# Delta rule with the inverse inside the scan, TensorE's order from an estimate of engine times, decays made in each batch

## The chip, the cores and the metric

The kernel runs on one core of one Trainium2 chip. The metric is device time in microseconds (us), the median of several executions. Five engines work side by side, each through its own queue in order: TensorE (PE, matmuls; its weight loads are shown as PEld), VectorE (DVE), ScalarE (ACT), GpSimd (POOL) and SyncE (SP, which here only issues DMAs).

## The reference: what is computed

Two layers over 1088 frames (1024 of a prompt, 64 of a running sample), width 1024, one set of weights. The even layer is a gated convolution beside chunk-band attention, the odd layer a gated DeltaNet with 8 heads of 128; each ends in an output projection, a norm and a residual sum. The change is in the odd layer's recurrence over chunks of 64 frames, and in the order of everything on TensorE.

```python
def gdn_chunk(S, q, k, v, g, beta):
    gc = jnp.cumsum(g, axis=1)
    decay = jnp.exp(jnp.where(incl, gct[..., :, None] - gct[..., None, :], -jnp.inf))
    kk = jnp.einsum('blhd,bmhd->bhlm', k, k)
    a = jnp.where(strict, bt[..., :, None] * kk * decay, 0.0)
    tmat = a + jnp.eye(L)
    rhs = concatenate([v * beta, k * (beta * jnp.exp(gc))])
    sol = triangular_solve(tmat, rhs, lower=True, unit_diagonal=True)
    u = sol[..., :HD_C] - jnp.einsum('bhlk,bhkv->bhlv', sol[..., HD_C:], S)
    qk = jnp.einsum('blhd,bmhd->bhlm', q, k) * decay
    o = jnp.einsum('blhk,bhkv->blhv', q * jnp.exp(gc), S) + jnp.einsum('bhlm,bhmv->blhv', qk, u)
    k_dec = k * jnp.exp(g_last - gc)
    S_new = jnp.exp(g_last) * S + jnp.einsum('blhk,bhlv->bhkv', k_dec, u)
    return S_new, o
```

## The kernel before

**Projections.** Weights come as 128-column tiles (`wf`, two DMAs of 256 KB each on SP's queue) and are split into a high and a low part (`whi` by ACT, line 161; `wlo` by DVE, line 162). `project` (line 172) runs, for each of the three groups of frames (384, 384, 320 columns) and each of eight slices of the width, three matmuls in the reduced-precision format fp32r on the whole 128 x 128 array; their output is the PSUM tile `pjt`. The program makes 5832 of these. Everything else on TensorE is plain fp32, of which the trace shows two records per matmul and one per transpose.

**The odd layer.** Heads go in four pairs. A pair's q, k and v columns are six weight tiles; `conv` (line 699) convolves them into `kq` and `vt`, two buffers each, so the projections of pair p wait until the scan of pair p-2 has ended (line 1168). The 17 chunks of a pair go in three batches of 6, 6 and 5. Per batch:

- `prepare` (855): loads the decays `Dst` and `DT` from DRAM (lines 869 and 870, SP's queue), transposes k and q, takes norms, and forms the strict matrix `An` and the masked product `KQD`.
- `substitute` (918): inverts the 16 x 16 diagonal blocks on POOL: 28 small steps (lines 930 and 931) between two trips through DRAM (`Sd` to `AL`, then `AL` to `Sd`).
- `join` (938): reads the blocks back (`Xf`), and builds the 64 x 64 inverse with matmuls of 16 and 32 columns on 32 x 32 corners of the array, each pair of heads into the block-diagonal `BD`.
- `solve` (1006): per chunk a transpose of v, a product of `kt` with `BD` and one of `BD` with v, all on the whole array.
- `scan` (1032): per chunk `ks` (four matmuls, weights of 64 columns: k and q of both heads against the state `S`), `us` on DVE, `su` (two matmuls over 64 rows), the new `S` on DVE, and later `up` (two matmuls on 64 x 64 corners) for the output.

Before all this `decays` (821) makes the decay matrices of all 12 batches, two POOL and two ACT steps and two stores to DRAM each, in a buffer `dbuf` that shares the two places of `vt`; the projections of pair 1 therefore stop at the line `yield "decays"` (1175) until all twelve are made.

**Order.** TensorE's instructions run in the order in which the program writes them. `Order` (line 75) holds the work as generators with a rank; it always takes the ready one of lowest rank (scan 1, solve 1.3, join 1.5, substitute 1.6, prepare 2, decays and the final norms 3, projections 5). A generator that has to wait for other engines yields a fixed number of nanoseconds; the clock against which this runs adds up estimated matmul times only. The order on the other engines is made by the compiler's scheduler.

Of the kernel before, what the change touches and what calls it, by code (L numbers as in the profile page):

```python
# [1 line left out]

# [13 lines left out]
P = 128  # L16
# [15 lines left out]
NBM = 6  # L32
# [41 lines left out]

class Order:
# [4 lines left out]
    def __init__(self):  # L80
        self.now = 0.0
        self.live = []
        self.done = set()

    def add(self, name, rank, steps, after=()):
        self.live.append([rank, len(self.live), name, steps, 0.0, set(after)])

    def run(self):
        while self.live:
            self.live.sort(key=lambda t: t[:2])  # L90
            free = [t for t in self.live if not (t[5] - self.done)]
            ready = [t for t in free if t[4] <= self.now]
            if not ready:
                self.now = min(t[4] for t in free)
                continue
            t = ready[0]
            try:
                w = next(t[3])
                if isinstance(w, str):
                    t[5].add(w)  # L100
                else:
                    t[4] = self.now + w
# [5 lines left out]
class Net:  # L108
    def __init__(self, tc, I, O):
        self.tc, self.nc, self.I, self.O = tc, tc.nc, I, O  # L110
        self.pe, self.act, self.dve, self.pool = tc.nc.tensor, tc.nc.scalar, tc.nc.vector, tc.nc.gpsimd
        self.order = Order()


    def mm(self, out, lhsT, rhs, start=True, stop=True, share=1, **k):
        n = out.free_size()
        four = 1 if lhsT.dtype == F32R else 4
        self.order.now += max(n, 60 if four == 1 else 16) * four / 2.4 / share + 3
        return self.pe.matmul(out, lhsT=lhsT, rhs=rhs, start=start, stop=stop, **k)  # L119

    def tr(self, out, in_):
        k = in_.partition_size()
        self.order.now += 108 if k > 64 else 56
        return self.pe.transpose(out, in_, self.ident[0:k, 0:k])  # L124

    def bank(self):
        p = self.banks[0]
        self.banks = self.banks[1:] + [p]
        return p.tile([P, 512], F32, name="pjt", tag="pj", bufs=2 if p is self.pj else 4)

# [41 lines left out]
    def project(self, w, ops, n, m=P, ks=range(KT)):  # L172

        ps = self.bank()
        ks = list(ks)
# [41 lines left out]
    def open(self, name, side="left", **k):  # L217
        es = ExitStack()
        p = es.enter_context(self.tc.tile_pool(name=name, bufs=1, **(dict(side=side, reuse_waits="tile") if not k else k)))
# [7 lines left out]
    def run(self):  # L227
# [4 lines left out]
        with tc.tile_pool(name="pj", bufs=2, space=PSUM) as self.pj:  # L232
# [15 lines left out]
            self.Dd = [dram.tile([P, NCH, 64], F32, name=f"Dd{i}") for i in range(8)]  # L248
# [44 lines left out]
    def norm(self, l, g, xin, y, acc, last):  # L293
# [4 lines left out]
        yield 1620  # L298
        r = self.rstd(tp, acc, n, None if l and g else last)
        yield 2500  # L300
        if l == 0:
            acc = tp.tile([P, GMAX], F32, name="sqb", tag="sqa", bufs=2)[:, :n]
        for m in range(KT):
# [11 lines left out]
            yield 1050  # L315
        if l == 0:
            nc.sync.dma_start(self.xd[:, :, t0:t0 + n], x[:, :, :n])
            yield 2500
            r = self.rstd(tp, [acc, sq], n, last)
            self.new_h(g)  # L320
            yield 2500
            for k in range(KT):
                self.h_tile(tp, 1, g, x, r, k)
                yield 1360
# [76 lines left out]
    def even(self):  # L401
# [7 lines left out]
        self.sc_free = 0.0  # L409
# [74 lines left out]
        def v_tokens(p):  # L484
            b = B[p]
            for i0, m in ((0, 4), (4, 4), (8, 1)):
# [785 lines left out]
```

## Time and profile before

| | us |
|---|---|
| median of 3 runs (lowest, highest) | 1501.44 (1500.14, 1503.16) |
| the profiled execution's own time | 1498.51 |
| its span, first to last instruction | 1496.7 |
| ACT whi, 222 casts / DVE wlo, 222 subtractions | 129.9 / 155.6 |
| scan matmuls of `ks` / `su` / `up`, busy | 42.7 / 33.5 / 29.6 |

The profile's windows give the time in which each engine worked in a stretch, and PEclk, the share of TensorE's full clock that was granted there. A wait names the instruction that ended it. Matmuls overlap: a row's busy time is the union of its records, so what one more matmul costs is read from the distance between starts in the timeline.

By the order of the program and the trace, the stages are: even layer to about 542 us (2304 projection matmuls), its output projection to about 652, the odd layer to about 1346, then the last gates and the output projection. The 68 chunks of the scan run from 834 to 1336, some 4.4 us apart where they follow one another.

### The profile page before, as it was taken

To read this page: it belongs to the slowest core of one execution; us is meant where nothing else is said; L and a number is where in the kernel's file an instruction comes from. 1 tells how busy PE (TensorE), PEld (TensorE's weight loads), DVE (VectorE), ACT (ScalarE), POOL (GpSimd) and SP (SyncE) were. 2 spreads that over 40 slices of the span, in tenths; PEclk is the share of its full clock that TensorE was granted. 3 is DMA by queue.
4 is the path that set the end of the run, shared out by engine and by line. 5 is a ranking of instruction groups with operands and counts; after the bars stand their busy time and mean duration, and the time that the engine had idled before them with its cause. 6 is when DMAs were issued, how large, how long until landed. Compare 5 with 4: busy or idle time off the path is not lost. (4 is left out here: it accounts for less than half of the span.)

```text
span 1496.7 us, 28755 instructions
## 1 busy us (share of the span) xinstructions
PE 1376.2 (92%) x10578; PEld 1237.4 (83%) x10578; DVE 858.7 (57%) x2400; ACT 745.6 (50%) x1948; POOL 402.1 (27%) x909
## 2 busy tenths in 40 slices
PE   4899999999999999898876999999989989999995
PEld 3888998999999899887765877778877778888985
DVE  6647237326525755776675667664756665443654
ACT  6544144235325456776655566556555644323642
POOL 4100000000000014432447254452645261410322
PEclk9999999999999999998987999999999999999998
DMA  5231210220211174541332112211211132337454
GB/s 201 83 114 44 77 58 26 87 65 29 74 61 58 44 233 149 180 146 36 94 87 63 31 51 57 42 41 47 67 35 41 37 96 60 99 108 238 154 190 156
DMA packets 114381, 133.15 MB, mean 89 GB/s; under 512 B 35568, under 2 KB 81336, under 8 KB 114240
## 3 DMA queue, kind: packets, MB, share of 16 engines
q1 hardware_dynamic: 82128, 101.86, 22.9%
q10 hardware_dynamic: 32112, 29.45, 6.1%
q8 instruction: 83, 1.36, 0.4%
q14 instruction: 58, 0.48, 0.1%
HBM read 99.91 MB, written 34.51 MB: 90 GB/s over the span
## 5 line engine op out<-in xcount | busy, mean ns | idle before, releaser
L119 PE MATMUL pjt<-hhi,wlo 128*128 128x384 f32 (+1 forms) x1768 | 621.4, 351 | 1.8 <-DVE wlo L162 1.8
L119 PE MATMUL pjt<-hhi,whi 128*128 128x384 f32 (+1 forms) x1768 | 587.5, 332 | 19.7 <-ACT ko L464 4.2
L119 PE MATMUL pjt<-hlo,whi 128*128 128x384 f32 (+1 forms) x1768 | 586.8, 332 | 7.3 <-DVE hlo L215 6.6
L119 PEld LDWEIGHTS pjt<-hhi,whi 128*128 128x128 f32 x1768 | 340.4, 193 | 29.1 <-ACT hhi L214 6.6
L119 PEld LDWEIGHTS pjt<-hhi,wlo 128*128 128x128 f32 x1768 | 340.3, 192 | 26.0 <-issue 12.2
L119 PEld LDWEIGHTS pjt<-hlo,whi 128*128 128x128 f32 x1768 | 339.0, 192 | 10.5 <-DVE hlo L215 8.8
L162 DVE TENSOR_TENSOR wlo<-wf,whi 128x512 fp32r<-128x512 f32 x222 | 155.6, 727 | 138.3 <-ACT whi L161 137.0
L161 ACT CAST whi<-wf 128x512 fp32r<-128x512 f32 x222 | 129.9, 619 | 154.7 <-PE pjt L119 110.9
L544 ACT ACTIVATE pr<-pr,mx 128x640 f32<-128x640 f32 (+5 forms) x72 | 50.9, 706 | 92.7 <-DVE mx L543 92.2
L722 POOL TENSOR_TENSOR kq<-kq,tap 128x384 f32<-128x384 f32 (+1 forms) x64 | 49.7, 784 | 140.5 <-DVE kq L719 99.5
L505 POOL MEMSET bias<- 64x64 f32 x8 | 1.5, 187 | 315.4 <-DMA bias<-Gd 245.0
L345 POOL TENSOR_TENSOR sqa<-sqa,sq 128x384 f32<-128x384 f32 (+1 forms) x36 | 39.7, 1103 | 150.1 <-ACT sq L343 150.0
L541 DVE CUSTOM_DVE_ANT_0 pr<-sc,bias 128x640 f32<-128x640 f32 (+5 forms) x72 | 48.0, 666 | 26.3 <-PE sc L119 22.8
L1093 DVE SCALAR_TENSOR_TENSOR S<-S,egl,su 128x128 f32<-128x128 f32 x128 | 41.1, 343 | 34.9 <-PE su L119 34.3
L930 POOL TENSOR_TENSOR px<-AL 48x14 f32<-48x14 f32 (+6 forms) x168 | 48.6, 289 | 40.0 <-DMA AL<-Sd 31.6
L931 POOL TENSOR_TENSOR AL<-AL,px 48x14 f32<-48x14 f32 (+6 forms) x168 | 52.4, 312 | 8.7
L719 DVE SCALAR_TENSOR_TENSOR kq<-raw,par,kq 128x384 f32<-128x384 f32 (+1 forms) x96 | 48.7, 526 | 9.9 <-ACT raw L715 9.7
L610 POOL TENSOR_TENSOR cvo<-cvo,th 128x384 f32<-128x384 f32 (+1 forms) x12 | 12.0, 999 | 142.6 <-DVE mx L543 113.3
L884 ACT ACTIVATE junk<-tr 128x128 f32<-128x128 f32 x136 | 38.0, 279 | 19.8 <-PE tr L124 16.5
L124 PE MATMUL pt<-cst,pr 128*128 128x128 f32 (+1 forms) x280 | 43.2, 270 | 4.4 <-DVE pr L546 2.9
L119 PE MATMUL pjt<-mhi,whi 128*128 128x384 f32 x128 | 43.5, 340 | 3.1 <-ACT mhi L161 3.1
L119 PE MATMUL pjt<-mlo,whi 128*128 128x384 f32 x128 | 43.7, 342 | 0.3 <-DVE mlo L162 0.3
(240 smaller groups left out, 2344.5 us busy)
## 6 DMA issues: line engine op xcount, KB each, us to landing
wf<-in_w_in SPq DMA_DIRECT2D x128, 256.0 KB, 3.2
wf<-in_w_out SPq DMA_DIRECT2D x96, 256.0 KB, 3.4
mf<-mixd SPq DMA_DIRECT2D x32, 192.0 KB, 3.5
x<-in_x SPq DMA_DIRECT2D x8, 384.0 KB, 5.3
xg<-in_x SPq DMA_DIRECT2D x2, 1536.0 KB
xd<-xg SPq DMA_DIRECT2D x2, 1536.0 KB, 6.9
Dd<-dbuf ACTq DMA_DIRECT2D x16, 192.0 KB, 2.2
od<-o ACTq DMA_DIRECT2D x12, 256.0 KB, 2.5
```

What stands on the lines that cost most here:

```text
L119: return self.pe.matmul(out, lhsT=lhsT, rhs=rhs, start=start, stop=stop, **k)
L124: return self.pe.transpose(out, in_, self.ident[0:k, 0:k])
L161: self.act.copy(out=hi, in_=x)
L162: (eng or self.dve).tensor_tensor(lo, x, hi.bitcast(F32), ALU.subtract)
L345: pool.tensor_tensor(acc, acc, sq, ALU.add)
L541: dve.tensor_tensor_reduce(out=cut(pr[0:nq, :nk]), in0=sc[0:nq, :nk // nw, :nw], in1=cut(b["bias"][a][0:nq, j0:j0 + nk]), scale=1.0, scala ...
L544: act.activation(pr[0:nq, :nk], pr[0:nq, :nk], AF.Exp, bias=mx[0:nq, 1:2], scale=1.0, accum_out=mx[0:nq, 2:3])
L719: dve.scalar_tensor_tensor(o, ch(raw[:, i0 + j:i0 + j + m]), cw[j], o, ALU.mult, ALU.add)
L722: pool.tensor_tensor(o, o, ch(t), ALU.add)
L930: pool.tensor_tensor(t, AL[:, j + 1:16, j:j + 1].broadcast_to([lanes, m, w]), x.broadcast_to([lanes, m, w]), ALU.mult)
L931: pool.tensor_tensor(o, o, t, ALU.add)
L1093: dve.scalar_tensor_tensor(Sn[:, q, :], S[:, q, :], egl[:, q, p, c:c + 1], su[q], ALU.mult, ALU.add)
```

## The change

1. **Order.** `Clock` replaces the fixed waits. While the program is recorded it is told of every instruction (`Meter` wraps the other engines, `Pool` the buffers), books it with a fixed and a per-column cost on its engine, and keeps for each part of a tile when it will be written or read for the last time. A generator now yields the tiles and buffer places that its next matmul needs and is ready when the estimate has passed them all, with 250 ns more for all but the projections. `project` yields between its matmuls too.
2. **Decays.** `decays`, its DRAM tensors `Dd`, the buffer `dbuf` and the stop of pair 1 go. `prepare` makes `Dst` and `DT` itself: the same matmul, two POOL and two ACT steps per batch. 24 stores on ACT's queue and 24 loads on SP's queue go.
3. **Solve.** `solve` goes; of it only the transpose of v is left (`values`). `join` makes the inverse in both orientations (`tr<-X,M` beside `tr<-M,X`), and a new product `tr<-KQD,Ti` on 64 x 64 corners, so that one matrix `MT` per chunk holds inverse and masked q-k product for both heads.
4. **Scan.** Three dependent matmul steps per chunk in place of two and a late one. `ks`: two matmuls on the whole array (k and q of one head stand side by side in `kq`). Then `r` (two DVE steps of 64 rows into a block-diagonal tile whose other half is zero), `uo` (one matmul of 256 columns), two ACT copies to the block-diagonal `u`, `su` (one matmul of 256 columns) and the new `S`. The output's first part is copied from `ks` by ACT, the second added from `uo` by DVE.

```diff
+class Clock:
...
+    FIXED = {"DVE": 170, "ACT": 210, "POOL": 260}
+    EACH = {"DVE": 1.04, "ACT": 0.84, "POOL": 1.9}
+    NEAR, PSUM, DMA, BYTES = 60, 190, 2000, 190.0
...
+    def tensor(self, out, ins, cost, shape, more):
+        t = max([self.now] + [self.ready(x) for x in ins] + ([] if more else [self.over(out, "PE", False)]))
+        if shape != self.shape:
+            t += 200
+            self.shape = shape
+        self.now = t + cost
...
+    def other(self, eng, op, outs, ins):
+        t = max([self.ready(x, eng) for x in ins] + [self.over(x, eng, False) for x in outs])
...
+            n = max(x.free_size() for x in outs[:1] + ins)
+            took = self.FIXED[eng] + self.EACH[eng] * n + (200 if len(outs) > 1 else 0)
+            at = self.place(eng, t, took)
...
 class Order:
...
+    LATE = 250
...
+    def due(self, t):
+        at = 0.0
+        for x in t[4]:
+            at = max(at, (x() if callable(x) else self.clock.ready(x)) + self.LATE * (t[0] < 5))
+        return at
...
     def project(self, w, ops, n, m=P, ks=range(KT)):
...
+        yield [self.bank_turn, w[0][:, ks[0], :], ops[0][ks[0]]]
         ps = self.bank()
...
             hi, lo = ops[0][k], ops[1][k]
+            yield [w[0][:, k, :], w[1][:, k, :], hi, lo]
             o = ps[0:m, :n]
             self.mm(o, w[0][:, k, :], hi, k == ks[0], False)
             self.mm(o, w[0][:, k, :], lo, False, False)
-            yield 0
+            yield ()
             self.mm(o, w[1][:, k, :], hi, False, k == ks[-1])
...
-            KQ[p] = k1.tile([P, 2, NCH, 2, 64], F32, name="kq", tag="kq", bufs=2)
+            KQ[p] = k1.tile([P, NCH, 2, 2, 64], F32, name="kq", tag="kq", bufs=2)
...
-        def decays():
...
         def prepare(p, b):
...
-            yield 4000 if b == 0 else 0
...
-            nc.sync.dma_start(Dst, Dd[2 * p][:, c0:c0 + nb, :])
-            nc.sync.dma_start(DT, Dd[2 * p + 1][:, c0:c0 + nb, :])
...
+            dve.tensor_tensor(Dst, gcb, cst[:, C_ID64:C_ID64 + 64].unsqueeze(1).broadcast_to(sh), ALU.mult)
+            yield [Dst, turn("tr")]
+            ps = pst("tr")[:, :64 * nb]
+            self.mm(ps, cst[:, C_BD:C_BD + P], Dst.rearrange("p c j -> p (c j)"))
+            dve.tensor_tensor(DT, ps.rearrange("p (c j) -> p c j", j=64), gcb, ALU.subtract)
+            for x, cm, op in ((Dst, C_M1, ALU.subtract), (DT, C_M2, ALU.add)):
+                pool.tensor_tensor(x, cst[:, cm:cm + 64].unsqueeze(1).broadcast_to(sh), DT, op)
+                act.activation(x, x, AF.Exp)
...
         def substitute(p, b):
...
-            yield 6500
+            yield [AL]
...
         def join(p, b):
...
-            yield 2250
+            yield [Cb, XT, turn("tr")]
...
                     self.mm(ps[r, i, :], X[r, i, :], M[r, i, :], share=1.5, tile_position=(64 * q, 64 * q))
+                    self.mm(ps[o, i, :], M[r, i, :], X[r, i, :], share=1.5, tile_position=(64 * q, 64 * q + 32))
...
+                    self.mm(ps[h, i, :], Ti[h, i, :], KQD[h, i, :], share=1.6, tile_position=(64 * q, 64 * q))
...
-        def solve(p, b):
+        def values(p, b):
...
-                    self.mm(ps[:, i, :], kt[:, i0 + i, :], BD[:, i0 + i, :])
...
-                    self.mm(ps[:, i, :], BD[:, i0 + i, :], vr[:, i, :])
...
         def scan(p, b):
...
+                    yield [S, kq[:, c], turn("ks")]
                     ks = pst("ks")
-                    for a in range(2):
-                        for q in range(2):
-                            self.mm(ks[64 * q:64 * q + 64, P * a:P * a + P], kq[:, a, c, q, :], S[:, q, :], share=1.6)
...
-                    dve.tensor_tensor(u, ks[:, 0:P], vt[:, c, :], ALU.add)
...
-                    yield 850
+                    for q in range(2):
+                        self.mm(ks[:, col[q]], kq[:, c, q].rearrange("p a t -> p (a t)"), S[:, q, :])
+                    for q in range(2):
+                        h = half[q]
+                        dve.scalar_tensor_tensor(r[h, q, :], ks[h, col[q]], kap[h, i:i + 1], vt[h, c, :], ALU.mult, ALU.add)
+                    for q in range(2):
+                        o = half[1 - q]
+                        act.activation(o4[o, a, :], ks[o, col[q]], AF.Copy, scale=egs[o, p, c:c + 1])
...
+                yield [flat(r), MT[:, i, :], turn("uo")]
+                uo = pst("uo")[:, 0:2 * P]
+                self.mm(uo, MT[:, i, :], flat(r))
                 for q in range(2):
...
+                    h = half[q]
+                    act.copy(out=u[h, q, :], in_=uo[h, col[q]])
...
+                        dve.tensor_tensor(o4[o, a, :], uo[o, col[q]], o4[o, a, :], ALU.add)
...
+                yield [flat(u), kd[:, i, :], turn("su")]
+                su = pst("su")[:, 0:2 * P]
-                    self.mm(su[q], kd[h, i, :], u[h])
+                self.mm(su, kd[:, i, :], flat(u))
...
-                yield 1110
...
-                order.add(f"wy{n}", 1.3, solve(p, b), [f"inv{n}", f"v{p}"])
+                order.add(f"vtr{n}", 1.3, values(p, b), [f"v{p}"])
...
-                    if p == 1:
-                        yield "decays"
```

What this does to the order is seen at three places. In the rows a name stands before the arrow for the tile written, behind it for those read; `pjt` rows are projections, and `xN` counts like rows in a stretch.

The first is a chunk of the scan of the first pair on TensorE. Before, one chunk is `ks`, `su` and the `up` that follows, in two places between groups of projections:

```order
L119 MATMUL up<-us,KQD 64x128 x2
L119 MATMUL ks<-S,kq 64x128 x4
L119 MATMUL pjt<-hhi_6901,wlo 128x320
L119 MATMUL pjt<-hhi_6035,whi 128x384
L119 MATMUL pjt<-hlo_6036,whi 128x384
L119 MATMUL pjt<-hhi_6035,wlo 128x384
L119 MATMUL pjt<-hhi_6035,whi 128x384
L119 MATMUL pjt<-hlo_6036,whi 128x384
L119 MATMUL su<-us,kd 128x128 x2
```

With the change, from the tenth chunk of the first pair on, the same engine has this; the tiles alternate between `r_7077` and `r_7079` from chunk to chunk:

```order
L278 MATMUL ks<-S,kq 128x128 x2
L278 MATMUL tr<-kq 64x128 x8
L278 MATMUL uo<-r_7079,MT 128x256
L278 MATMUL tr<-kq 64x128 x4
L278 MATMUL su<-u_7083,kd 128x256
L278 MATMUL ks<-S,kq 128x128 x2
L278 MATMUL uo<-r_7077,MT 128x256
L278 MATMUL su<-u_7081,kd 128x256
L283 MATMUL tr<-cst,o_9173 128x128 x4
L278 MATMUL ks<-S,kq 128x128 x2
L278 MATMUL uo<-r_7079,MT 128x256
L278 MATMUL su<-u_7083,kd 128x256
```

Each chunk has three places instead of two, and here no projection stands between them. In all, 31 such steps of the scan (`ks`, `uo` or `su`) follow one another without a projection at the end of pair 0, 14 at the end of pair 1 and 21 at the end of pair 2; before, the longest such stretch has 6 (`up`, `ks`, `su` twice). The numbers of projections passed there are 3816, 4248 and 4680, at which the projections wait for a scan to free its buffers.

The second is ScalarE where pair 0 ends and pair 1 begins; its copies to `u` now stand between `uo` and `su`:

```order
L186 COPY u_7081<-uo 64x128 x2
L186 ACTIVATE junk,ss<-tr 128x128
L186 ACTIVATE Dst<-Dst 128x320
L186 ACTIVATE junk,ss<-tr 128x128 x2
L186 ACTIVATE DT<-DT 128x320
L186 ACTIVATE junk,ss<-tr 128x128
L186 COPY kd<-tr 64x512
L186 ACTIVATE junk,ss<-tr 128x128 x4
L186 COPY kd<-tr 64x512
L186 ACTIVATE o_10130<-ks,egs 64x128 x2
L186 COPY u_7083<-uo 64x128 x2
```

`u` and the output's part from `ks` are new on this engine, and `prepare`'s squares, copies and exponentials of the decays stand in the same queue between two chunks.

The third is TensorE at the end of the even layer, the last unit of attention (`sc` scores, `pt` transposes, `pv` product with v). Before, its last rows have projections between them:

```order
L124 MATMUL pt<-cst,pr 128x64 x4
L119 MATMUL pjt<-hhi_170,wlo 128x384
L119 MATMUL pjt<-hhi_177,whi 128x320
L119 MATMUL pjt<-hlo_178,whi 128x320
L124 MATMUL pt<-cst,pr 128x64 x4
L124 MATMUL pt<-cst,pr 64x64 x2
L119 MATMUL pjt<-hhi_177,wlo 128x320
```

Now all that could be put there has been used before it:

```order
L278 MATMUL pv<-ptS,vtok 64x128 x10
L278 MATMUL sc<-ks,qs 64x288
L278 MATMUL sc<-klo,qs 64x288
L278 MATMUL sc<-ks,qs 64x288
L278 MATMUL sc<-klo,qs 64x288
L278 MATMUL sc<-ks,qs 64x288
L278 MATMUL sc<-klo,qs 64x288
L278 MATMUL sc<-ks,qs 64x288
L278 MATMUL sc<-klo,qs 64x288
L283 MATMUL pt<-cst,pr 128x64 x8
L283 MATMUL pt<-cst,pr 64x64 x2
L278 MATMUL pv<-ptS,vtok 64x64 x10
```

Scores, transposes and product of this unit now follow one another, and the projections come behind them.

More of the change, by code (lines that the diff above doesn't have):

```diff
@@ new lines, with __init__, __getattr__, call @@
+class Meter:
+    def __init__(self, clock, eng, real):
+        self._clock, self._eng, self._real = clock, eng, real
+    def __getattr__(self, name):
+        real = getattr(self._real, name)
+        if not callable(real):
+            return real
+        def call(*a, **k):
+            r = real(*a, **k)
+            aps = {i: x for i, x in enumerate(a) if hasattr(x, "tensor")} | {i: x for i, x in k.items() if hasattr(x, "tensor")}
+            outs = [aps.pop(i) for i in ("out", "accum_out") if i in aps]
+            if aps and (not outs or "out" not in k):
+                first = next(iter(aps))
+                outs.insert(0, aps.pop(first))
+            if outs:
+                self._clock.other(self._eng, name, outs, list(aps.values()))
+            return r
+        return call
@@ L90, in run @@
             self.live.sort(key=lambda t: t[:2])
-            free = [t for t in self.live if not (t[5] - self.done)]
-            ready = [t for t in free if t[4] <= self.now]
+            free = [(t, self.due(t)) for t in self.live if not (t[5] - self.done)]
+            ready = [t for t, at in free if at <= self.clock.now]
             if not ready:
-                self.now = min(t[4] for t in free)
+                self.clock.now = min(at for _, at in free)
                 continue
@@ L109, in __init__ @@
     def __init__(self, tc, I, O):
-        self.tc, self.nc, self.I, self.O = tc, tc.nc, I, O
-        self.pe, self.act, self.dve, self.pool = tc.nc.tensor, tc.nc.scalar, tc.nc.vector, tc.nc.gpsimd
-        self.order = Order()
-    def mm(self, out, lhsT, rhs, start=True, stop=True, share=1, **k):
-        n = out.free_size()
-        four = 1 if lhsT.dtype == F32R else 4
-        self.order.now += max(n, 60 if four == 1 else 16) * four / 2.4 / share + 3
+        self.tc, self.I, self.O = tc, I, O
+        self.clock = Clock()
+        self.pe = tc.nc.tensor
+        self.act, self.dve, self.pool, sync = (Meter(self.clock, e, x) for e, x in (
+            ("ACT", tc.nc.scalar), ("DVE", tc.nc.vector), ("POOL", tc.nc.gpsimd), ("SP", tc.nc.sync)))
+        self.nc = SimpleNamespace(scalar=self.act, vector=self.dve, gpsimd=self.pool, sync=sync)
+        self.order = Order(self.clock)
+    def mm(self, out, lhsT, rhs, start=True, stop=True, share=1, **k):
+        n, rows, cols = out.free_size(), lhsT.partition_size(), lhsT.free_size()
+        if lhsT.dtype == F32R:
+            cost = max(n / 2.4 + 14, 108)
+        else:
+            cost = max(4 * n / 2.4 + 14, 60 if rows < 64 else 220) / share
+        self.clock.tensor(out, [lhsT, rhs], cost, (-(-rows // 32), -(-cols // 32)), not start)
         return self.pe.matmul(out, lhsT=lhsT, rhs=rhs, start=start, stop=stop, **k)
@@ L122, in tr @@
         k = in_.partition_size()
-        self.order.now += 108 if k > 64 else 56
+        self.clock.tensor(out, [in_], 109 if k > 64 else 62, (-(-k // 32), 4), False)
         return self.pe.transpose(out, in_, self.ident[0:k, 0:k])
@@ L1156, in odd @@
                         order.add("gates", 2, gates(ba))
-                        order.add("decays", 3, decays(), ["gates"])
                     continue
```

336 lines of the change are left out of this document (198 added, 138 removed).

## The prediction

> **What bounds the kernel now.** I read the page's head first, then the windows, then who TensorE waits for in the odd layer, then the timeline of one chunk.
>
> ```profile
> span 1496.7 us, 28755 instructions
> PE 1376.2 (92%) x10578; PEld 1237.4 (83%) x10578; DVE 858.7 (57%) x2400; ACT 745.6 (50%) x1948; POOL 402.1 (27%) x909
> ```
>
> TensorE works 92% of the span and no other engine over 57%: a gain must shorten its work, or end an idle time of it. The windows say where that idle time is (PE first, PEclk after POOL):
>
> ```profile
> 60.00:542.00 482.00, 471.32 (x3259) 447.06 (x3258) 238.56 (x667) 189.65 (x450) 15.15 (x29) 0.99 0.23 72
> 690.00:1310.00 620.00, 562.30 (x5385) 474.36 (x5384) 386.63 (x1322) 337.99 (x1059) 279.07 (x766) 0.96 0.22 57
> 772.00:830.00 58.00, 39.43 (x344) 34.77 (x344) 31.58 (x81) 29.09 (x70) 34.22 (x80) 0.82 0.30 63
> 830.00:1060.00 230.00, 218.44 (x2215) 178.83 (x2215) 146.62 (x557) 134.73 (x443) 99.70 (x296) 1.00 0.19 46
> ```
>
> In the even layer (60 to 542) TensorE idles 11 us of 482: nothing to win there. In the odd layer (690 to 1310) it idles 620 - 562.3 = 57.7 us, and the clock was 0.96, which is at most 620 x 0.04 = 25 us more. The part from 772 to 830 alone idles 19 us at a clock of 0.82; that is where the projections are held until the decays are made. What the idle times waited for:
>
> ```profile
> PE tr L119 <- DVE XT L960: 12.2, 3, 9.3
> PE tr L124 <- DVE o L1114: 7.2, 3, 5.3
> PE tr L124 <- DVE KQD L906: 5.9, 4, 2.2
> PE tr L124 <- DVE dbuf L838: 5.4, 2, 3.7
> ```
>
> They are waits of the preparing steps (`XT` of `join`, `KQD`, `dbuf` of the decays), few and long, not of the scan.
>
> **TensorE's work.** The timeline of one chunk, PE only, start and length:
>
> ```profile
> 1000.64 0.34 PE L119 MATMUL pjt<-hlo,whi 128*128 128x384 f32 x1
> 1000.91 0.44 PE L119 MATMUL up<-us,KQD 64*64 64x128 f32 x4
> 1001.28 0.66 PE L119 MATMUL ks<-S,kq 128*64 128x128 f32 x8
> 1001.86 0.44 PE L119 MATMUL pjt<-hhi,wlo 128*128 128x384 f32 x1
> 1002.14 0.34 PE L119 MATMUL pjt<-hhi,whi 128*128 128x384 f32 x1
> ...
> 1002.84 0.34 PE L119 MATMUL pjt<-hlo,whi 128*128 128x384 f32 x1
> 1003.11 0.49 PE L119 MATMUL su<-us,kd 64*128 64x128 f32 x4
> 1003.53 0.44 PE L119 MATMUL pjt<-hhi,wlo 128*128 128x384 f32 x1
> 1003.81 0.34 PE L119 MATMUL pjt<-hhi,whi 128*128 128x384 f32 x1
> ...
> 1025.32 0.34 PE L119 MATMUL pjt<-hlo,whi 128*128 128x384 f32 x1
> 1025.50 0.38 PE L119 MATMUL tr<-vr,BD 128*128 128x128 f32 x2
> 1025.64 0.42 PE L119 MATMUL pjt<-hhi,wlo 128*128 128x384 f32 x1
> 1025.90 0.34 PE L119 MATMUL pjt<-hhi,whi 128*128 128x384 f32 x1
> ```
>
> Projections start some 0.175 us apart. From the last one before `up` to the second one behind `ks` are 1.50 us; without two normal steps, `up` with `ks` costs 1.15. In the same way `su` costs 0.97 - 0.35 = 0.62. A chunk of the scan costs 1.77. The last four rows are the counterexample that I lean on: `tr<-vr,BD`, plain fp32 on the whole array, costs 0.58 - 0.35 = 0.23 for two records of 128 columns, just its stream, while the step into `su` takes 0.27 and the step after it 0.28 in place of 0.175. So it is not fp32 that costs at the border but the cut array.
>
> The Trainium skill ("TensorEngine Tiling (Array Packing)", Key Properties) says that changing the tiling mode drains TensorE; the rows agree. The same page (When to Use Tiling) asks for 2x row tiling where the contraction is 64 or less, up to twice as fast, and the change does the opposite, padding 64 rows with zeros: by that rule `su` would have run at half of what the new one takes, some 0.2 us a chunk or an estimated 15 us lost on 68. The row of `su` speaks against it: its four records take 0.42 us, as long as 256 columns on the whole array.
>
> *Scan.* New per chunk: `ks` two matmuls of 128 columns, `uo` and `su` one of 256 each, all on the whole array, at 0.23 per 128 columns six times: 1.38. Saved 0.39 on some 66 chunks: 26 us; if the records come at 0.107, as 384 columns stream, 0.49 each or 32. I take 29.
>
> *Solve.* Two products of 128 columns go, in each of 68 chunks:
>
> ```profile
> L119 PE MATMUL tr<-BD,kt 128*128 128x128 f32 x136 | 19.9, 281 | 2.7 <-DVE KQD L906 1.1 <-DVE BD L1002 0.9 <-ACT vr L1018 0.7
> L119 PE MATMUL tr<-vr,BD 128*128 128x128 f32 x136 | 19.5, 278 | 0.6 <-ACT o L1122 0.6
> L119 PE MATMUL tr<-M,X 32*32 32x32 f32 x272 | 6.7, 193 | 0.0
> ```
>
> 272 records at 0.11 are 30 us; the busy sum of 39 is the other bound.
>
> *Join.* `tr<-KQD,Ti` has no row. The nearest is `up`, the same corners with twice the columns: 0.37 a chunk. Half of that is 13 us on 68, all of it 25; with 12 borders at 0.2 I take 16 (13 to 28). `tr<-X,M` doubles the third row: 7 us (nothing, if it runs beside the other corner, to 13).
>
> *Borders.* The order shows 196 steps from a projection into a cut array before and 70 now; 109 of them belong to `up` and `su`, which are counted above. The rest at 0.2 gives 3 us.
>
> *Decays.* Their matmul, POOL and ACT steps stay, per batch. 48 DMAs go from SP's and ACT's queues, where weights and outputs stand behind them; DMA is busy 0.2 to 0.3 of these windows, so I take nothing.
>
> Sum of the work: 29 + 30 + 3 - 16 - 7 = **39 us less** (25 to 50).
>
> **Waits.** The 57.7 us of the odd layer go with the fixed waits, and of the 25 of the clock some 18, the rest being idle anyway: 76. What is late instead:
>
> *The scan without cover.* In the new order 66 steps of the scan follow one another without a projection (31, 14 and 21 at the ends of pairs 0, 1 and 2), because more projections are put between the first chunks and they run out. There a step costs its matmul, the reader's work and the next start. Rows for these:
>
> ```profile
> 1264.53 0.66 PE L119 MATMUL ks<-S,kq 128*64 128x128 f32 x8
> 1265.23 0.29 DVE L1079 TENSOR_TENSOR us<-ks,vt 128x128 f32<-128x128 f32 x1 [0.24 <-PE ks L119]
> ...
> 1261.63 0.49 PE L119 MATMUL su<-us,kd 64*128 64x128 f32 x4
> 1262.56 0.34 DVE L1093 SCALAR_TENSOR_TENSOR S<-S,egl,su 128x128 f32<-128x128 f32 x1
> L1081 ACT ACTIVATE qs<-ks,egc 128x128 f32<-128x128 f32 x64 | 23.4, 366 | 25.6 <-DVE us L1079 23.9 <-issue 0.2
> ```
>
> From `ks` to the end of `us` are 0.99 us, and a second DVE step adds 0.2: 1.2. From `su` to the second `S` are 1.27. `uo` to `u` is 0.46 of stream, some 0.25 of tail as behind `ks`, and two ACT copies, for which 0.37 and another 0.25 stand: 1.33. With the hand-over a mean of 1.35 without anything in the way. But behind `u` wait the next `su` and all of TensorE's queue, and ahead of it ACT has casts and squares; I take 1.5 (1.25 to 2.0). 66 x 1.5 = 99 us. TensorE's own work there is 62 us, an estimate: 28 for the 66 steps at their stream of 0.43, the rest for 111 transposes and some 370 small products that the order puts between them, at the distances that such records have in the timeline. Idle: **37** (20 to 70).
>
> *`XT`.* `substitute` runs through DRAM and POOL:
>
> ```profile
> 1219.50 3.55 DMA Sd<-AL
> 1223.11 3.02 DMA Xf<-Sd
> L930 POOL TENSOR_TENSOR px<-AL 48x14 f32<-48x14 f32 (+6 forms) x168 | 48.6, 289 | 40.0 <-DMA AL<-Sd 31.6
> L931 POOL TENSOR_TENSOR AL<-AL,px 48x14 f32<-48x14 f32 (+6 forms) x168 | 52.4, 312 | 8.7
> ```
>
> 28 POOL steps at 0.3 are 8.4 us, four such DMAs 12 to 13, and the steps around them 2: 22 to 23 from the last `tr<-kq`. The new order leaves 9, 17, 12 and 16 us of TensorE's work in four of the twelve batches (the fourth, fifth, seventh and tenth). They lack 35 together, but lie in the stretches above, whose idle time covers most of it: **8** (0 to 25).
>
> *Clock.* Stretches that idle a third lose clock, as 772 to 830 does at 0.82: 99 us at some 0.9: **10** (0 to 28).
>
> *Other waits.* The stretch 830 to 1060 idles 5% although well covered. Over the remaining some 480 us that would be 24; I take **20** (5 to 30), the margins being 0.25 us over an estimate.
>
> Together 75 against 76: **the waits move, and gain 1 us**.
>
> *End of the even layer.* The last attention unit has lost its cover (the third place in the order). One score buffer, the chain through DVE and ACT:
>
> ```profile
> L541 DVE CUSTOM_DVE_ANT_0 pr<-sc,bias 64x576 f32<-64x576 f32 x8 | 6.0, 749 | 4.9 <-PE sc L119 4.8
> L544 ACT ACTIVATE pr<-pr,mx 64x576 f32<-64x576 f32 x8 | 6.2, 778 | 18.0 <-DVE mx L543 18.0
> ```
>
> 0.75 before the second scores, then 0.75 + 0.78 + some 1.0 of small steps, then the copies: 4 us, less than 1 of clock behind it. **5 more** (2 to 8).
>
> Sum: 1498.5 - 39 - 1 + 5 = 1463.5 against the profiled execution's own time; the median shown lies 2.9 above that, so **1466 us**.
>
> **Rivals.**
>
> 1. *The estimate is right* and the uncovered steps cost 1.25, nothing waits for `XT`, the clock stays up: waits 20 + 0 + 0 + 12 in place of 75, so 43 less: 1423, with the work's margin 1430. For it: `us` and `S` hardly made TensorE wait before (they are not among the waits above). Against it: there six or nine projections stood in front of each.
> 2. *Half clock in the uncovered stretches.* The matmul in each step doubles from 0.45: 66 x 0.45 = 30 us less the 10 counted, and some of the `XT` wait: 1466 + 26 = 1492. The Trainium skill ("TensorE: Matmul & The Clock Gate", HAM oscillation) has TensorE fall back after idle of about 3.4 us, and describes another case where micro-idles suffice. By the first, steps of 1.5 us with 0.9 of work keep the clock; by the second, not. Here 830 to 1060 kept 1.00 with short waits, 772 to 830, with waits up to 9.3 us, did not, which leans to the first.
> 3. *Slower: three legs in place of two.* The chain of scan steps becomes the bound, with ACT's queue in it. At 2.2 us a step the stretches take 145 us instead of 99, with 8 more of `XT` and 5 of clock: 1466 + 59 = 1525. It decides from the point where 35 us are lost, that is 1.5 + 35/66 = 2.03 us a step. For it: ACT carries `prepare`'s squares and copies between two chunks, as the order shows, in its own queue. Against it: by the rows of `us` and `S` a step is 1.0 to 1.3 us where the engine is free.
> 4. *The saving in work isn't there:* 256 columns with zeros drain as the cut array does, and `KQD,Ti` costs its bound: 39 becomes about 4, and the time 1501, no change.
>
> **How the numbers follow.** Forecast 0.48, rival 1 0.17, rival 2 0.11, rival 4 0.07, rival 3 0.17. Faster by over 0.2% (about what a measurement tells from no change): 0.76; same: 0.07; slower: 0.17. The range runs from rival 1 with the larger saving (1420) to short of rival 3's point (1515), where half of rival 3 still lies inside.
>
> **What would show it.** Right: busy time of `ks`, `uo` and `su` with even starts and no gap of 0.27 at their borders; no wait for `dbuf`; three stretches without `pjt` near the ends of pairs 0 to 2, of some 46, 21 and 32 us, with `r`, `u` and `S` as their releasers; the windows before and after at 95% or more. Wrong: stretches of over 130 us together, or `XT` waits of over 25 us, or, on the other side, no more than 40 us idle in the whole odd layer.

## The result, and the profile after

The changed kernel takes **1613.9 us** (median of 4 runs, 1611.0 to 1617.9) beside 1500.8 (1499.2 to 1503.2): ratio 1.075, 95% interval 1.072 to 1.079. It is slower by 113 us, outside the range. The profiled execution took 1616.7 us.

The page of the changed kernel, with span, TensorE's row and the granted clock by fortieths of the span:

```profile
span 1614.9 us, 28798 instructions
PE 1415.8 (88%) x10326; PEld 1289.2 (80%) x10326; DVE 909.1 (56%) x2588; ACT 817.3 (51%) x2161; POOL 407.5 (25%) x997
PEclk9999999999999899989998758997779858999998
```

There are 252 matmul records fewer and yet 40 us more busy time: in nine of the twelve slices from the 23rd to the 34th the clock is 5 to 8 tenths, and a matmul at half clock is busy for twice as long (`uo` 1.19 us in place of 0.59, in the rows further down). The windows of the odd layer (PE first, PEclk behind POOL; the sum is that of 690 to 1460); the three stretches in which no projection runs are the second, fourth and sixth row:

```profile
830.00:892.00 62.00, 57.32 (x583) 51.87 (x583) 44.25 (x143) 38.40 (x112) 32.44 (x92) 0.92 0.18 36
892.00:973.00 81.00, 53.61 (x431) 36.07 (x430) 46.33 (x188) 39.47 (x143) 31.84 (x121) 0.62 0.10 23
973.00:1095.00 122.00, 110.79 (x957) 102.70 (x957) 79.16 (x271) 78.17 (x235) 49.58 (x133) 0.93 0.14 33
1095.00:1142.00 47.00, 28.48 (x290) 19.96 (x288) 24.42 (x97) 23.20 (x81) 16.15 (x54) 0.62 0.14 27
1142.00:1275.00 133.00, 114.58 (x950) 104.01 (x950) 77.83 (x270) 74.73 (x226) 53.08 (x151) 0.88 0.12 30
1275.00:1338.00 63.00, 38.33 (x310) 25.59 (x309) 31.98 (x122) 27.89 (x97) 29.28 (x101) 0.60 0.15 38
...
sum 770.00, PE 640.07 PEld 558.36 DVE 455.37 ACT 430.20 POOL 295.64; mean PE 80.01 PEld 69.79 DVE 56.92 ACT 53.78 POOL 36.96
```

These three stretches are called bare below. They take 81 + 47 + 63 = 191 us. TensorE idles 191 - 120.4 = 70.6 us in them, at a clock of 0.6.

**Three sums.** Adding up the trace between the first and the last matmul: idle time; the distances between starts of successive matmuls without the idle time, those at half clock halved ("work at full clock"); and that other half ("half-clock excess").

| kernel | profiled, us | idle | half-clock excess | work at full clock | 56 chunk distances inside batches | 11 at batch starts |
|---|---|---|---|---|---|---|
| before | 1498.5 | 98.0 | 28.0 | 1347.8 | 272 | 230 |
| change | 1616.7 | 176.0 | 106.2 | 1309.1 | 534 | 97 |
| a: new math, fixed waits | 1595.3 | 179.3 | 75.5 | 1315.1 | 491 | 131 |
| b: old math, estimate | 1537.4 | 124.0 | 48.8 | 1339.0 | 279 | 245 |
| c: decays in batch alone | 1534.7 | 120.5 | 38.7 | 1349.5 | 291 | 272 |
| n: c tuned | 1509.3 | 103.2 | 31.7 | 1348.5 | 281 | 256 |
| o: a tuned | 1574.3 | 167.4 | 66.5 | 1314.2 | 458 | 141 |
| q: o with two legs | 1565.6 | 169.1 | 58.0 | 1312.7 | 368 | 215 |

The work saved is there, 38.7 us. It is lost four times over: 78 us more idle and 78 us more of half-clock excess. The last two columns (distances between the first `su` of successive chunks) say how: before, the scan ran in bursts of some 4.5 us a chunk (the median) and then waited at batch starts, 230 us in all, for the preparing steps. Now its chunks take 534 us, and 97 us are left at the batch starts.

### The profile page after: what moved, and what is told of

It reads as the page before. It is cut to its first block, busy times and chain, and to the rows that moved or that the text cites. A ratio compares the mean times of both kernels' runs of the same rounds, so it can differ in the third digit from the quotient of the medians.

```text
span 1614.9 us, 28798 instructions
## 1 busy us (share of the span) xinstructions
PE 1415.8 (88%) x10326; PEld 1289.2 (80%) x10326; DVE 909.1 (56%) x2588; ACT 817.3 (51%) x2161; POOL 407.5 (25%) x997
## 4 chain that ended last, share of the span: by engine, by line
PE 49%; DVE 14%; DMA 13%; ACT 10%; POOL 8%; issue 6%; ACTq 0%; SPq 0%; DVEq 0%; POOLq 0%
PE pjt L278 36%; DMA out_convC<-raw 4%; PE pv L278 2%; PE tr L278 2%; PE sc L278 2%; PE pt L283 2%; POOL AL L186 2%; POOL px L186 2%; POOL so L186 2%; DMA wf<-in_w_out 2%; ACT junk L186 2%; ACT whi L186 2%; DMA Sd<-Af 1%; DVE wlo L186 1%; PE uo L278 1%
## 5 line engine op out<-in xcount | busy, mean ns | idle before, releaser
L278 PE MATMUL pjt<-hhi,whi 128*128 128x384 f32 (+1 forms) x1768 | 608.2, 344 | 18.2 <-ACT raw L186 4.0
L278 PE MATMUL pjt<-hhi,wlo 128*128 128x384 f32 (+1 forms) x1768 | 613.0, 347 | 4.6 <-DVE wlo L186 4.4
L186 ACT ACTIVATE o<-ks,egs 64x128 f32<-64x128 f32 x128 | 46.4, 363 | 76.5 <-DVE r L186 63.0
L278 PE MATMUL uo<-r,MT 128*128 128x256 f32 x136 | 55.1, 494 | 23.5 <-DVE r L186 18.3
L186 POOL TENSOR_TENSOR so<-so 128x4 f32<-128x4 f32 (+2 forms) x216 | 47.7, 221 | 89.9 <-DVE so L186 77.4
L186 DVE SCALAR_TENSOR_TENSOR r<-ks,kap,vt 64x128 f32<-64x128 f32 x128 | 44.5, 347 | 41.9 <-PE ks L278 40.5
L278 PE MATMUL ks<-S,kq 128*128 128x128 f32 x256 | 52.1, 335 | 17.9 <-DVE S L186 11.4
L186 DVE TENSOR_TENSOR o<-uo,o 64x128 f32<-64x128 f32 x128 | 36.9, 289 | 53.8 <-ACT u L186 51.4
L278 PEld LDWEIGHTS ks<-S,kq 128*128 128x128 f32 x256 | 43.6, 231 | 26.6 <-DVE S L186 16.2
L278 PE MATMUL su<-u,kd 128*128 128x256 f32 x136 | 54.7, 491 | 6.9 <-ACT u L186 6.8
```

Of the source, the lines that this page charges most:

```text
L186: r = real(*a, **k)
```

## The experiments

All ratios are to the kernel before on the same chip, and "us above" is the distance of the two medians; the change is 113 above. A leg is one matmul step of the scan with the step of another engine that reads it.

**One part at a time (a to d).** Run a keeps the new `join`, `values`, `scan` and in-batch decays but makes the order as before; run b is the old math under `Clock`; run c moves the decays alone; run d changes how the estimate books the scan's readers.

```diff
 # a: each yield of tiles becomes a number
-                yield [flat(r), MT[:, i, :], turn("uo")]
+                yield 1050
 # b: each number becomes a yield of tiles
-                    yield 850
+                yield [u, kd[:, i, :], turn("su")]
 # c: in prepare of the kernel before
-            nc.sync.dma_start(Dst, Dd[2 * p][:, c0:c0 + nb, :])
+            dve.tensor_tensor(Dst, gcb, cst[:, C_ID64:C_ID64 + 64].unsqueeze(1).broadcast_to(sh), ALU.mult)
+            yield 900
...
-                        yield "decays"
 # d: in Clock.other, own is set around r, u and S
-            at = self.place(eng, t, took)
+            at = self.place(eng + "own" if self.own else eng, t, took)
```

> The changed join, values, scan and in-batch decays, but TensorE's order made as before, by fixed waits in ns (850 behind ks became 1050 for two VectorE steps, 1110 behind uo and behind su). In this order only one stretch of 6 scan steps has no projection, in place of 31, 14 and 21. Theory ORDER (the estimate puts 20 to 79 projections into single chunks, so the scan's chain becomes the bound and the projections run out): near the blind forecast, 1460 to 1505 us, chunks some 5 us apart, granted clock of the scan stretch 0.95 or more. Theory LEGS (three dependent legs whose readers stand in VectorE's and ScalarE's queues are too long in any order): 204 legs wait 0.5 to 0.7 us each for a late reader, 100 to 140 us, so 1570 us or more, idle TensorE all through the scan.

> The old decays, solve and two-legged scan, with TensorE's order from the estimate of engine times (part 1 of the change alone). No scan step stands without projections near it. ORDER, if the estimate is bad whatever it orders: 1530 to 1600 us, chunks 6 us apart and more. LEGS: the estimate is harmless and takes away the fixed waits, 1450 to 1490 us.

> The kernel before with its decays made inside prepare and no stop at pair 1 (part 2 alone), all else as it was. Both theories: faster by the 19 us of idle TensorE that the stretch 772 to 830 held and some 5 of clock, less what the longer prepare delays: 1475 to 1495 us. Slower than 1501 would mean that part 2 adds its steps to a chain that sets the end.

> The changed kernel, but the estimate books r, u and S of the scan on tracks of their own, as if no other work stood before them on VectorE and ScalarE: legs are estimated at 1.1 to 1.4 us and the order puts some 5 to 8 projections into each in place of up to 40. Bare stretches fall from 66 scan steps to 26. ORDER: 1480 to 1560 us. LEGS: the legs stay as long as their readers' queues make them, TensorE idles in front of them instead of running projections, 1590 us or more.

Measured: a 1595.2 us (1.059, 1.055 to 1.064; 91 above); b 1544.1 (1.027, 1.022 to 1.032; 40); c 1538.7 (1.024, 1.020 to 1.028; 35); d 1576.5 (1.048, 1.044 to 1.052; 73). Order and decays each lose by themselves, and c, from which both theories expected a gain, loses 35 us. The new math was run only together with the in-batch decays; run a lies 56 us above c. Run a, on the side of LEGS, says that the old way of ordering isn't the cure; but my port (the new math written for fixed waits) put the transposes of v right behind the last projection of v with no wait, and 19.5 us of its idle time are that. Run d lies between: booking the readers without a queue brings 40 us. The stretches of over 8 us without a projection in its odd layer fall from 190 to 64 us, yet TensorE still idles 168 us in all (176 in the change), now 28.8 us before `su` for `u`, 19.4 before `uo` for `r` and 13.1 before `ks` for `S`. So late readers cost time in legs with projections too.

Where c loses is in its waits of TensorE:

```profile
PE tr L124 <- DVE o L1095: 36.0, 8, 12.2
PE tr L119 <- DVE Dst L844: 13.9, 4, 6.1
```

The first is the output norm: before, it made TensorE wait 7.2 us. Its small steps `so` run on GpSimd.

**Is it GpSimd's queue (e, f, g)?** The same edit in runs c and b and in the change:

```diff
-            rsqrt(fa, va, tm, pool)
+            rsqrt(fa, va, tm, dve)
```

> Run c with the square root of the output norm (the last steps so of finish) on VectorE instead of GpSimd. Theory GPSIMD QUEUE: in run c TensorE stood 36.0 us in 8 waits before tr<-o, because the small steps so stand in GpSimd's queue behind X, which waits for its DMA, behind substitute's steps and now behind the decays' Dst and DT of 0.99 us each; on VectorE these waits fall to about the 7 us of the kernel before, and the half clock that follows long waits goes with them: 1538.7 - 29 - 10 = about 1500, range 1485 to 1515. Rival, DECAYS ON THE CHAIN: the in-batch decays lengthen prepare itself, other waits take the place of these: 1525 to 1540.

> Run b with the same step on VectorE. GPSIMD QUEUE: 28.5 us of tr<-o waits in run b, the longest 8.7, fall to 7 or less, with some 10 us of half clock: 1544 - 32 = about 1512, range 1500 to 1525. Rival, ESTIMATE: the order itself is bad and the wait only shows where it is late: 1535 or more.

> The changed kernel with the same step on VectorE. GPSIMD QUEUE: 21.5 us of tr<-o waits go, but 6 of 7 lie in or near the bare scan stretches whose chain is the bound: 1614 - 10 to 25, so 1590 to 1605. THREE LEGS: the chain of legs sets the time, the new steps on VectorE stand before r and S there: 1605 to 1625.

Measured: e 1534.5 us (1.021, 1.016 to 1.026; 32 above); f 1547.1 (1.031, 1.026 to 1.036; 44); g 1614.2 (1.074, 1.071 to 1.077; 112). The theory falls: in e the wait is still 27.0 us, now behind other steps of VectorE; in g it grows from 21.5 to 26.7. What makes the norm late is not shown.

**Is it the clock (h)?** Matmuls that nobody reads, behind each leg while the projections are held:

```diff
+                if any(t[2] == "main" and t[5] - order.done for t in order.live):
+                    f = self.pj.tile([P, 512], F32, name="fill", tag="pj", bufs=2)
...
+                    for j in range(6):
+                        self.mm(f[:, 0:GMAX], h[:, j % KT, 0:P], h[:, j % KT, :])
```

> The changed kernel with six matmuls of 384 columns, whose result nobody reads, behind each scan leg while the projections are held: some 350 of them, 61 us of TensorE's time at full clock, laid into the idle and half-clock time of the three bare stretches (191 us in all). CLOCK (half clock makes the bare legs 2.9 us long in place of some 2.2): the granted clock there rises from 0.61 to 0.9 and the stretches shorten by 30 to 50 us: 1565 to 1585. QUEUES (readers late in VectorE's and ScalarE's queues set the legs): the clock rises and the time stays, 1605 to 1630.

Measured: 1595.9 us (1.062, 1.058 to 1.065; 93 above). Windows of run h over its three stretches:

```profile
894.00:967.00 73.00, 61.83 (x579) 54.05 (x577) 43.84 (x180) 37.68 (x139) 25.20 (x98) 0.98 0.10 23
1095.00:1135.00 40.00, 33.48 (x357) 29.52 (x355) 22.01 (x85) 24.14 (x82) 18.33 (x57) 0.87 0.15 27
1270.00:1310.00 40.00, 33.38 (x357) 29.36 (x356) 23.42 (x86) 23.63 (x79) 19.27 (x63) 0.87 0.19 49
```

The clock comes back and the stretches shrink from 191 to 153 us, as CLOCK expected, but the whole gains only 20: other waits grow (`tr<-o` to 35.7 us). By the sums above, 52 us of half-clock excess are left (106 in the change, 28 before), and the 348 added matmuls put 62 us of work into TensorE's order. So 20 us is what giving back some 54 us of half clock in this way was worth; what the clock alone costs of the 113 stays open.

**Table loads and written waits (i to l).** ScalarE loads its function table at each change between Exp and Silu, 1.28 us each. Rows of run c, whose decays (L851) and Silu (L728) alternate:

```profile
L728 ACT ACT_TABLE_LOAD x10 | 12.8, 1283 | 0.2
L851 ACT ACT_TABLE_LOAD x10 | 12.8, 1283 | 0.2
```

```diff
 # i, k, l: conv
-            half = ti % 8 < 2
+            half = True
 # j, k: prepare, finish
-            yield 900
+            yield 3000
-            yield 9000
+            yield 16000
```

> Run c with the convolutions' Silu written as tanh for all pairs (as it is already for pair 0), for one more VectorE step per projection group (54 of 0.54 us). Run c loads ScalarE's function table 36 times, the kernel before 20: Exp of the decays now alternates with Silu. TABLE LOADS: some 16 loads of 1.28 us go from ScalarE's queue, where the scan's and the norm's steps stand behind them; 10 to 20 us of the 35 come back: 1515 to 1530 us. Rival, OTHER QUEUES (GpSimd and the waits as written): within 5 us of 1538, or slower for the VectorE steps.

> Run c with two fixed waits of the order lengthened, 900 to 3000 ns in front of tr<-Dst and 9000 to 16000 ns in front of the output norm's transposes tr<-o. FIXED WAITS TOO SHORT: the 13.9 and 36.0 us in which TensorE stood before these two in run c are filled with projections, and half clock behind them goes: 1495 to 1515 us. Rival: the norm that comes later holds the scan (three buffers o4) or other waits take their place: 1525 to 1545.

> Both edits of the two runs beside it on run c. If each answers for its own part: 1475 to 1500 us, faster than the kernel before, since the idle of the stop at pair 1 is gone. If there is one chain behind both: as the better of the two.

> The changed kernel with tanh in place of Silu: its table loads fall from 32 to some 20, 12 x 1.28 = 15 us of ScalarE's queue, in which u stands. TABLE LOADS on the scan's chain: 1590 to 1605 us. THREE LEGS: the order stays as it is made from the estimate, and with more VectorE work in front of r and S the time is 1610 to 1630.

Measured: i 1539.9 us (1.026, 1.023 to 1.029; 37 above); j 1543.9 (1.028, 1.025 to 1.031; 41); k 1514.0 (1.008, 1.006 to 1.010; 11); l 1610.6 (1.072, 1.070 to 1.075; 107). Run i has 18 loads fewer than c and not a microsecond to show for it, but also 54 VectorE steps more, which make that engine 30 us busier; run j only moves its waits (`tr<-XT` 23.3 us). Both together win 24 us over c. I had expected the two to answer for separate parts; neither did. In the change itself the same swap gains some 6 us, VectorE's steps included.

**The third leg (m), and tuned versions (n, o, p).**

```diff
 # m
-                yield [flat(u), kd[:, i, :], turn("su")]
...
-                self.mm(su, kd[:, i, :], flat(u))
+                yield [kd[:, i, :], turn("su")]
...
+                self.mm(su, Z["no"], flat(r))
 # n (on k), o (on a with the edits of k), p (on before, with 16000 for the norm)
-            yield 6500
+            yield 7000
-            yield 2790
+            yield 4000
-            yield 2250
+            yield 3000
```

> The changed kernel with the state's matmul su taking r in place of u, against a zero matrix in place of kd: it leaves out the state's update (a chunk then only decays S), but not an instruction; only the leg uo to u is off the chain from one chunk to the next. THREE LEGS (the chain of 204 legs of some 3 us is the bound, and 68 of them go): bare stretches of 191 us shrink to 100 or less and the time falls by 60 to 110 us, 1505 to 1555. Rival, PREPARING STEPS (the batches' own chain, prepare to substitute to join, and queues make the stretches long): 1585 or more.

> Run k (in-batch decays, tanh, longer waits for Dst and the norm) with the waits around substitute and in join lengthened too (6500, 2790, 2250 to 7000, 4000, 3000 ns), since run k stood 19.1 us before XT, 10.8 of them at the first batch. If the waits as written are what part 2 lost by: 1490 to 1505 us, at or below the kernel before. Rival, the batches' chain: later joins make the scan late and the time stays at 1510 or grows.

> Run a (new join, values and scan under fixed waits) with the edits of run n: tanh, and the longer waits. THREE LEGS: what the waits cost comes back as in run k, 25 to 40 us, and the chain stays: 1550 to 1575, still 50 or more above run n. ORDER (the waits were all that was wrong): within 15 us of run n or below it, since TensorE has some 40 us less work.

> The kernel before with the longer waits of run n around substitute, in join and for the norm, its decays and Silu as they are. It stood 12.2 us before XT and 7.2 before tr<-o. If longer waits help by themselves: 1485 to 1495. If they only move the wait: within 5 us of 1503.

Measured: m 1574.5 us (1.045, 1.042 to 1.049; 71 above); n 1510.5 (10 runs; 1.006, 1.003 to 1.008; 7); o 1574.3 (1.046, 1.042 to 1.051; 71); p 1523.2 (1.013, 1.008 to 1.017; 20). Taking the third leg out of the chain brings 42 us, between the two expectations. The new math costs 64 us more than the old under the same waits (o against n), though it has 34 us less work; 24.4 us of run o's idle time are again the wait of my port before the transposes of v. And p shows how far the written waits of the kernel before are fitted: "safer" ones cost it 20 us.

**What the 64 us are (q, r).**

```diff
 # q: as m, on o, and without the wait behind uo
-                yield 1110
 # r: on o
-                yield 1050
+                yield 700
-                yield 1110
+                yield 800
...
-                yield 1110
+                yield 700
```

> Run o with the leg uo to u taken out of the chain as in run m (su reads r against a zero matrix, so the state's update is left out; no instruction is), and without the 1110 ns behind uo. THREE LEGS: the 64 us between runs n and o are the third leg's, chunks fall from 27 projections to 18, the chain has slack again: 1500 to 1525. Rival, NEW JOIN AND READERS (the new join, the halved r and u steps and the norm's share of the queues): 1545 or more.

> Run o with the three waits of the scan shortened, 1050, 1110, 1110 to 700, 800, 700 ns, so 15 to 18 projections stand in a chunk in place of 27. READERS LATE (three legs of at least 1.8 to 2.2 us each with the readers' queues): TensorE stands before r, u and S, 30 to 60 us more idle there, and the time stays at 1560 to 1590. WAITS TOO LONG: chunks of 5 us, no chain, 1520 to 1545.

Measured: q 1564.4 us (1.041, 1.038 to 1.043; 61 above); r 1579.3 (1.051, 1.049 to 1.053; 76). In r TensorE stands before `r` (30.2 us), `u` (21.9) and `S` (14.5): with shorter waits the readers set the pace, as READERS LATE expected. In q the chain has slack again (215 us at batch starts), and the time falls by 10 us only, as the rival had it. Its waits:

```profile
PE tr L124 <- DVE vt L725: 33.2, 8, 5.4
PE ks L119 <- DVE S L1091: 16.3, 14, 3.2
PE tr L119 <- DVE Dst L848: 11.2, 2, 5.9
```

The first row is the fault of my port, which a, o, q and r share; under `Clock` that wait is 8.8 us. So the 54 us of q over n hold some 33 us, and the half clock behind them, that the change has only to a quarter (8.8 us). What the new `join` and the halved readers cost by themselves **stays open**; a port without that wait wasn't tried.

No version here beats the kernel before; run n, with the decays in the batch, comes nearest, at +0.6%.

## Why the prediction was wrong

**The work: right, its parts less so.** -39 was predicted, -38.7 is the sum of the trace. Taken one at a time the parts come out otherwise: the new math and decays under fixed waits save 32.7 (run a; 36 was predicted for all but the borders), and the order alone saves 8.8 (run b; 3 for the borders). So that the sum fits so closely is in part luck. Two places of the scan between projections in the changed kernel, PE only:

```profile
1400.49 0.33 PE L278 MATMUL pjt<-hlo,whi 128*128 128x384 f32 x1
1400.66 0.59 PE L278 MATMUL uo<-r,MT 128*128 128x256 f32 x2
1400.91 0.53 PE L278 MATMUL pjt<-hhi,wlo 128*128 128x384 f32 x1
1401.27 0.34 PE L278 MATMUL pjt<-hhi,whi 128*128 128x384 f32 x1
...
1411.18 0.33 PE L278 MATMUL pjt<-hhi,wlo 128*128 128x384 f32 x1
1411.36 0.61 PE L278 MATMUL ks<-S,kq 128*128 128x128 f32 x4
1411.72 0.42 PE L278 MATMUL pjt<-hhi,whi 128*128 128x384 f32 x1
1411.97 0.34 PE L278 MATMUL pjt<-hlo,whi 128*128 128x384 f32 x1
```

Read as in the prediction, `uo` costs 0.78 - 0.35 = 0.43 and `ks` 0.79 - 0.35 = 0.44. Three such steps are 1.31 in place of 1.77; 1.38 was predicted. The step into each is 0.17 or 0.18 us, as between projections, where the cut array of `su` before took 0.27; rival 4 is out.

**The bare stretches: the step that failed.** "66 x 1.5 = 99 us" measured 191, 2.9 us a step, beyond the 130 that the prediction gave as a sign of being wrong. The estimate of work in them was about right: 120.4 us busy at a clock near 0.6 are some 74 at full clock (62 was the prediction's estimate). But they idle 70.6 us, where 37 were predicted, and the clock, for which I allowed 10 us in all, adds some 46 to the rest. Of one chunk, the scan's own rows and what stood ahead of `r` in VectorE's queue:

```profile
913.27 0.75 PE L278 MATMUL ks<-S,kq 128*128 128x128 f32 x4 [0.89 <-DVE S L186]
913.40 0.15 DVE L186 SCALAR_TENSOR_TENSOR sA<-sT,kap 128x6 f32<-128x6 f32 x1
...
913.67 0.85 DVE L186 SCALAR_TENSOR_TENSOR An<-tr,sA,Dst 128x64 f32<-128x64 f32 x4
914.44 0.42 DVE L186 TENSOR_TENSOR KQD<-tr,DT 128x256 f32<-128x256 f32 x1
914.77 0.47 DVE L186 SCALAR_TENSOR_TENSOR An<-tr,sA,Dst 128x64 f32<-128x64 f32 x2
915.15 0.29 DVE L186 TENSOR_TENSOR KQD<-tr,DT 128x128 f32<-128x128 f32 x1
...
915.42 0.71 DVE L186 SCALAR_TENSOR_TENSOR r<-ks,kap,vt 64x128 f32<-64x128 f32 x2
...
916.27 1.19 PE L278 MATMUL uo<-r,MT 128*128 128x256 f32 x2 [2.25 <-DVE r L186]
...
917.50 0.53 ACT L186 COPY u<-uo 64x128 f32<-64x128 f32 x2 [0.54 <-PE uo L278]
...
918.09 1.22 PE L278 MATMUL su<-u,kd 128*128 128x256 f32 x2 [0.62 <-ACT u L186]
```

`ks` is done at 914.0; `r` starts at 915.4, behind `prepare`'s steps of the next batch in VectorE's queue. TensorE idles 2.25 us, falls to half clock at 915.3, and `uo` and `su` then take 1.2 us in place of 0.6. I had named the queues ("ahead of it ACT has casts and squares") and allowed 0.15 us a step for them. Over all 200 legs of the trace the reader starts 1.1 us after the start of its matmul's last record in the mean, where 0.3 to 0.4 is the least; I had charged such a delay to the 66 bare legs alone.

**"The waits move, and gain 1 us": wrong by 78 us of idle time and 78 of clock.** `XT`: 6.3 us, 8 predicted. The 76 us that I let go with the fixed waits did not go: run b, with the estimate's order and the old scan, has hardly a bare stretch (one of 12 us), and yet idles 124.0 us in place of 98.0, with 48.8 of half-clock excess in place of 28.0. And "other waits 20" was read from a stretch of the old scan, in which no leg was late. Outside the bare stretches the windows from 690 to 1460 idle 129.9 - 70.6 = 59 us. The longest waits of the whole run:

```profile
PE tr L283 <- DVE o L186: 21.5, 7, 6.3
PE tr L283 <- ACT kd L186: 20.5, 11, 5.2
PE uo L278 <- DVE r L186: 18.3, 18, 3.3
PE ks L278 <- DVE S L186: 11.4, 12, 3.0
...
PE tr L283 <- ACT vt L186: 8.8, 5, 3.3
```

Of these, `o` stands mostly outside the bare stretches (16.0 us of it in the windows from 690 on); of the others only 7.3 (`kd`), 3.7 (`r`), 6.1 (`S`) and 0.6 (`vt`) do. For `o` the order is at work. From one chunk with projections, PE and the readers:

```profile
1013.12 0.59 PE L278 MATMUL su<-u,kd 128*128 128x256 f32 x2
...
1013.75 0.61 DVE L186 SCALAR_TENSOR_TENSOR S<-S,egl,su 128x128 f32<-128x128 f32 x2 [0.54 <-PE su L278]
...
1018.37 1.02 DVE L186 TENSOR_SCALAR o<-o,so 128x128 f32<-128x128 f32 x4
...
1018.91 1.09 PE L283 MATMUL tr<-cst,o 128*128 128x128 f32 x4 [4.32 <-DVE o L186]
...
1022.99 1.05 PE L278 MATMUL ks<-S,kq 128*128 128x128 f32 x4
```

`S` is ready at 1014.4, but in TensorE's order stand 18 projections and the norm's transposes before the next `ks`, and the norm is 4.3 us late: one leg of 9.9 us. In this leg the order is wrong to both sides, too late for `S` and too early for `o`, and it is fixed before the run. In legs outside the bare stretches 1.0 to 1.7 us pass in the mean between a reader's end and the next leg (batch starts left out).

**The end of the even layer: right in size.** From the 145th to the 2305th projection 485.8 us in place of 482.4, +3.4 (5 predicted); the output projection behind it, not predicted, +4.5.

**The rivals.** Rival 1 is out: a bare step took 2.9 us, not 1.25. Rival 3 (three legs, ScalarE's queue in them, slower from 2.03 us a step) named the right side, and run m gives the third leg 42 us. Its price was too low, 1525, because I charged only the bare steps: the chain had some 180 us of slack at batch starts (230 less eleven chunks of 4.5) that no term of mine mentions, and with the longer legs 97 of the 230 are left. That the projections, which wait for the scan of the pair two back, then have to wait too is argued from these sums. Rival 2 is real: the clock in the bare stretches was 0.6, and run h, which gave back about half of the half-clock excess, gained 20 us. The decays, which I took as free to move, cost 35 us alone (run c).

What is shown is this: order and decays each lose when taken singly (b, c), and the new math loses on top of the decays (a); in the changed kernel the third leg is worth 42 us (10 under the waits of run o), the estimate's booking of the scan's readers 40, filling half-clock time 20, tanh in place of Silu 6. These overlap and don't add up to 113. Why order and decays lose by themselves, and how much the new `join` adds, is open.

## What to carry to other kernels

Before adding a dependent step to a chain, sum what slack the chain has, batch by batch, and price the step as matmul plus reader plus the queue ahead of the reader; here 38.7 us less work on the busiest engine bought nothing once the chain had become the bound. An order of instructions that is fixed beforehand holds only for the durations it was fitted to: here even longer safety waits cost 1.3%, and decays moved by a few steps 2.4%. How such an estimate should book the readers of a chain is not settled: with no queue at all (run d) it did better by 40 us than by fitting each step into the next gap of its engine, and one that serves each queue strictly in order wasn't run.

## What the hardware showed that was not expected

- **Half clock without long gaps.** From 935.7 on the clock stayed at half for 41 us:

```profile
936.00:976.00 40.00, 30.09 (x272) 20.75 (x273) 24.12 (x98) 15.69 (x64) 16.62 (x61) 0.50 0.09 21
```

  TensorE was busy for 75% of it, and after the first wait (5.2 us, up to 938.5) none was longer than 1.9 us. In the prediction I leaned on the first reading of the Trainium skill's page "TensorE: Matmul & The Clock Gate" (HAM oscillation: no idle gap beyond about 3.4 us). This fall lies within the wait of 5.2 us and agrees with that reading. Others disagree: at 870.9 the clock fell after a wait of 1.74 us and at 915.3 within one of 2.25, with no longer wait in the 12 us before. And once down it stayed down for 41 us with short gaps alone, while the stretches of run h, 84 to 85% busy, had a clock of 0.87 to 0.98.
- **A table load is its 1.28 us and no more.** The Trainium skill ("ScalarE: Activation LUTs", What ACT_TABLE_LOAD costs) adds a drain of about 1.4 us. Here, in the changed kernel, a copy ended at 932.83, the load ran from 932.84 to 934.12, and the next activation began at 934.14. In 25 of the 31 loads that follow another instruction, the next one begins 11 or 12 ns behind the load in this way.
